# Feed-forward projections as seven products of half matrices instead of eight, in a float32 decoder block

## The chip, the cores and the metric

The kernel runs on one core of a Trainium2 chip. Its metric is the time of one execution on the device, in microseconds (us), as the median of several runs. All data are float32; the tensor engine multiplies them as two float32r parts each, a high one (hi) and the rest (lo).

## The reference

A decoder block for 512 tokens of width 2048: differential attention and a convolution branch, merged by gates; then a feed-forward block of hidden width 5632; then a gated input embedding and a last norm. What the change touches is the feed-forward block and what stands on both sides of it:

```python
        x = x + merged @ w_o[l]
        h = _rmsnorm(x, g_ffn[l])
        u = _causal_dwconv(h @ w_up[l], ffn_conv_w[l], ffn_conv_b[l])
        ug, uv = jnp.split(u, 2, axis=-1)
        x = x + (jax.nn.silu(ug) * uv) @ w_down[l]
        h = _rmsnorm(x, g_ple[l])
        x = x + jax.nn.sigmoid(h @ w_ple_gate[l]) * (p[l].astype(x.dtype) @ w_ple_proj[l])
```

`w_up` is 2048 x 11264, `w_down` 5632 x 2048, and the convolution has three taps along the tokens.

## The kernel before

Activations lie with features on the 128 partitions and the 512 tokens along the free dimension, so a tile is 128 x 512. A weight comes in chunks of 256 x 512 (two blocks of 128 rows side by side, a tile of 128 x 1024 called `wraw`, three buffers). For each chunk `prep` writes the float32r high part with ScalarE (L223, `whi`) and the rest with VectorE (L224, `wlo`, the difference of two tiles in SBUF). Activations are parted the same way by `split` (L118 to L125). A product of a weight block with an activation tile is three matmuls of 512 columns (`products`, L274, L284): hi by hi, hi by lo, lo by hi. A chunk is 2 x 4 such products, so 24 matmuls, into four PSUM banks (`m`).

`run` (L203) walks over all chunks in one order: it issues the load of the chunk three ahead (`LD`), the split of the chunk two ahead (`LP`), then the 24 matmuls, and after a group's last chunk the eviction. Generators that are registered as background work (`add_bg`, `chain`) are pushed on by `pump` once for each chunk. Each engine works through its own queue in order; a scheduler may move instructions a little within it. All DMAs go through SyncE's queue, in the order in which the code issues them (L90).

The feed-forward block (L689 to L752) goes over the hidden width in four parts (`PARTS`). In each part come first the groups of `w_up` (two gate tiles and two value tiles to a group, 8 chunks), then those of `w_down` for that part. `ev_ffn` scales the four banks by the norm's factor (L538), convolves them (L699 once, L701 twice for each tile), applies SiLU (L705), multiplies (L706) and splits the result into the operands of the down products, which stay on chip. `ev_part` adds each part's down product to the residual, on chip too (L718). In all this is 22 groups of 8 chunks for `w_up` and 22 x 4 chunks for `w_down`. The products with `w_proj` stand before the last four down groups. GpSimd does a few constants and a power of a 128 x 4 tile for each norm (L164); nothing else.

Of the kernel before, what the change touches and what calls it, by code (L numbers as in the profile page):

```python
# [31 lines left out]
LD, LP = 3, 2  # chunks that the loads and the splits run ahead  # L32
# [21 lines left out]
class Group:  # L54
    """Products with a block of a weight, K x (128 nm), for the tokens ns; tok: tokens on the output's partitions."""
# [8 lines left out]

class Kernel:
    def __init__(self, tc, ctx, t):
        self.tc, self.nc, self.t = tc, tc.nc, t
        pool = lambda name, bufs, **k: ctx.enter_context(tc.tile_pool(name=name, bufs=bufs, **k))
        self.const = pool("const", 1)
        self.slots = pool("slots", SLOTS)  # L70
        self.wraw = pool("wraw", 3)
# [16 lines left out]

    def load(self, out, in_):
# [25 lines left out]
    # ---- exact split of a float32 tile into two float32r parts  # L115
# [21 lines left out]
    def colsum(self, acc):  # L137
        """[128 feat, 512 tok] -> [128 tok, 4] sums over the partitions."""
# [13 lines left out]
    def colsum_now(self, acc, js):  # L152
        """The same for some of the four blocks, by the shortest way."""
# [6 lines left out]
    def rsqrt(self, ss, scale, eps, n=4):  # L160
# [4 lines left out]
        # one step of Newton's iteration  # L165
# [12 lines left out]
    def bcast(self, r, n=4):  # L178
        """[128 tok, 4] -> [128, 512 tok], the same on every partition."""
# [22 lines left out]
    # ---- the stream of weight chunks  # L202
    def run(self, groups):  # L203
        nc = self.nc
        chunks = [(g, c) for g in groups for c in range(g.n)]
        raws, preps, tiles = {}, {}, {}

        def dma(i, kks=(slice(0, 2),)):
            if i < len(chunks):
                g, c = chunks[i]  # L210
                if i not in raws:
# [3 lines left out]

        def prep(i, kks=(slice(0, 2),)):
            if i >= len(chunks):
                return
            (g, c), raw = chunks[i], raws[i]
            n = g.nm * P  # L220

            def cut(hi, lo, w):
                nc.scalar.activation(hi, w, AF.Copy)  # L223
                nc.vector.tensor_tensor(lo, w, hi.bitcast(F32), op=ALU.subtract)  # L224

# [13 lines left out]
        loadx = self.start(dma, prep)  # L239
        for i, (g, c) in enumerate(chunks):  # L240
            for _ in range(2):
                next(loadx, None)
            dma(i + LD)
            prep(i + LP)
            raws.pop(i, None)
            tiles.pop(i, None)
            if c == 0:
                if g.before:
                    g.before()
# [13 lines left out]
        # the last columns for the other tokens, with the weights that are still here  # L263
        g = self.again
        for m in range(g.nm):
# [6 lines left out]
            g.evict(m, g.ps[m])  # L272

# [12 lines left out]
    # ---- start: the first tiles of x and of the weight, then the constants  # L286
    def start(self, dma, prep):
# [6 lines left out]
        # products of zeros until the first tiles are here: the tensor engine starts at a lower clock  # L294
# [22 lines left out]
        for i in range(1, LD):  # L317
# [38 lines left out]
        # lambda  # L356
# [108 lines left out]
    # ---- conformer convolution  # L465
# [44 lines left out]
    # ---- the whole block  # L510
    def build(self):
# [38 lines left out]
        def heads(h0, z):  # L550
            """The parts of queries and keys, stacked on the partitions: (qh, ql) against (kh, kh) and (kl, kl)."""
# [31 lines left out]
        # gated linear unit of the convolution branch  # L583
# [12 lines left out]
        # gates and branches  # L596
# [49 lines left out]
        # output projection, residual, next norm  # L646
        self.x1, self.hs = {}, {}
        xr = {}

        def load_res(mg):  # L650
            def f():
                if mg == 0:
                    self.finish_chains()
                for m in range(4 * mg, 4 * mg + 4):
                    xr[m] = self.A()
                    self.load(out=xr[m], in_=t["xT"][:, m, :])
            return f

        def ev_res(src, mg, dst, hs, gcol, last):
            """dst = src + product; its squares, and its split times the next norm's gain."""  # L660
            def chain():
                for m in range(4 * mg, 4 * mg + 4):
                    self.nacc = self.square_add(dst[m], self.nacc)
                    hs[m] = self.split(dst[m], self.col(gcol + m))
                    yield
                if mg == 3:
                    yield from last()
            def f(ps):
                for m in range(4):
                    z = src[4 * mg + m]  # L670
                    nc.vector.tensor_tensor(z, ps[m], z, op=ALU.add)  # L671
# [201 lines left out]
```

## Time and profile before

| | us |
|---|---|
| median of 3 runs (2853.17 to 2853.89) | 2853.4 |
| span of the profiled execution | 2851.3 |
| busy: TensorE (PE), its weight loads (PEld) | 2833.7, 2354.3 |
| busy: VectorE (DVE), ScalarE (ACT), GpSimd (POOL) | 1427.3, 907.9, 16.8 |
| feed-forward stretch of the chain that ended last | 1223.8 to 2671.1 |

The span goes from the first to the last instruction on the core; the profiled execution has no time of its own beside it, and the median lies 2.1 us above it. Times of parts of the kernel are read within the span. An engine's busy time is a sum of its instructions' durations, in which overlaps count once; a matmul's own duration (388 ns) is longer than the distance to the next one, since matmuls overlap in the array, so the rate is read from stretches of the chain.

### The profile page before, as it was taken

What the parts mean: (1) busy time and instruction counts of PE and PEld (TensorE: products, weight loads), DVE (VectorE), ACT (ScalarE), POOL (GpSimd) and SP (SyncE); (2) the same over time, 40 slices, a digit from 0 to 9 for tenths busy, and PEclk for the clock granted to TensorE, in tenths of its full rate; (3) what the DMA queues carried; (4) which work ended last, traced back from release to release, by engine and by line L of the source; (5) the groups of instructions that cost most, each with busy time, mean ns of one, the idle gap of its engine ahead of it and who ended that gap; (6) DMA issues with size and microseconds to landing.
All of it is one profiled execution on the core that took longest, in us unless ns stands there. A gap on an engine that the chain in (4) does not pass through costs nothing.

```text
span 2851.3 us, 31442 instructions
## 1 busy us (share of the span) xinstructions
PE 2833.7 (99%) x12824; PEld 2354.3 (83%) x12824; DVE 1427.3 (50%) x2035; ACT 907.9 (32%) x1291; POOL 16.8 (1%) x24
## 2 busy tenths in 40 slices
PE   9999999999999999999999999999999999999997
PEld 7888888888888888888888888888888888888887
DVE  5564687578455443445543345433445433455535
ACT  5354542222133222323321223221233212235333
POOL 0000000000000000000000000000000000000000
PEclk9999999999999999999999999999999999999999
DMA  5333322222222233322222222232222222223232
GB/s 191 111 104 104 97 81 96 96 96 97 97 95 96 98 126 116 112 96 97 96 97 96 96 96 97 98 99 98 96 96 96 96 96 97 97 96 108 94 109 82
DMA packets 86721, 288.27 MB, mean 101 GB/s; under 512 B 9776, under 2 KB 13872, under 8 KB 86576
## 3 DMA queue, kind: packets, MB, share of 16 engines
q1 hardware_dynamic: 86432, 286.25, 30.5%
q8 instruction: 100, 1.64, 0.2%
q14 instruction: 45, 0.37, 0.0%
q10 hardware_dynamic: 144, 0.01, 0.0%
HBM read 275.74 MB, written 4.19 MB: 98 GB/s over the span
## 4 chain that ended last, share of the span: by engine, by line
PE 99%; DMA 0%; DVE 0%; SPq 0%; ACT 0%; issue 0%; POOLq 0%; POOL 0%; DVEq 0%; ACTq 0%
PE m L284 97%; PE x L420 1%; PE x L393 0%; PE x L394 0%; PE x L411 0%; DMA wraw<-w_in 0%; PE x L132 0%; PE x L436 0%; DMA out<-o 0%; SPq L90 0%; DVE o L795 0%; PE x L188 0%; DVE wlo L224 0%; PE x L157 0%; ACT whi L223 0%
## 5 line engine op out<-in xcount | busy, mean ns | idle before, releaser
L284 PE MATMUL m<-a,whi 128*128 128x512 f32 (+1 forms) x7840 | 2403.7, 388 | 0.0
L284 PEld LDWEIGHTS m<-a,whi 128*128 128x128 f32 x7840 | 1467.0, 188 | 300.4 <-DVE a L538 0.3
L284 PE MATMUL m<-a,wlo 128*128 128x512 f32 (+1 forms) x3920 | 1520.0, 388 | 0.0
L224 DVE TENSOR_TENSOR wlo<-wraw,whi 128x1024 fp32r<-128x1024 f32 (+1 forms) x504 | 616.0, 1222 | 1207.7 <-ACT whi L223 1183.1
L223 ACT ACTIVATE whi<-wraw 128x1024 fp32r<-128x1024 f32 (+1 forms) x504 | 533.1, 1058 | 1657.1 <-PE m L284 1511.4
L284 PEld LDWEIGHTS m<-a,wlo 128*128 128x128 f32 x3920 | 736.0, 188 | 151.0 <-DVE wlo L224 0.3
L477 DVE SCALAR_TENSOR_TENSOR a<-a,par 128x485 f32<-128x485 f32 (+19 forms) x240 | 172.5, 733 | 6.1 <-ACT a L474 1.6
L538 DVE TENSOR_TENSOR a<-m,a 128x512 f32<-128x512 f32 x152 | 102.9, 691 | 52.4 <-PE m L284 52.4
L701 DVE SCALAR_TENSOR_TENSOR a<-a,par 128x510 f32<-128x510 f32 (+1 forms) x176 | 120.0, 744 | 0.0
L284 PE MATMUL m<-whi,a 128*128 128x512 f32 x256 | 81.2, 391 | 0.0
L120 ACT ACTIVATE a<-a 128x512 fp32r<-128x512 f32 x88 | 54.4, 620 | 45.1 <-DVE a L175 23.6
L699 ACT ACTIVATE a<-a,par 128x512 f32<-128x512 f32 x88 | 66.3, 801 | 0.0
L121 DVE TENSOR_TENSOR a<-a 128x512 fp32r<-128x512 f32 x88 | 60.2, 686 | 7.6 <-ACT a L120 7.0
L284 PEld LDWEIGHTS m<-whi,a 128*128 128x128 f32 x256 | 48.1, 189 | 10.2 <-ACT whi L223 0.6
L705 ACT ACTIVATE a<-a 128x512 f32<-128x512 f32 x44 | 27.9, 633 | 82.5 <-DVE a L701 82.5
L284 PE MATMUL m<-wlo,a 128*128 128x512 f32 x128 | 50.0, 390 | 0.2 <-DVE wlo L224 0.2
L398 ACT ACTIVATE a<-a,sm 128x128 f32<-128x128 f32 (+3 forms) x64 | 35.4, 554 | 19.8 <-DVE sm L396 19.8
L718 DVE TENSOR_TENSOR a<-m,a 128x512 f32<-128x512 f32 x48 | 32.8, 692 | 15.7 <-PE m L284 15.7
L199 DVE TENSOR_TENSOR a<-a 128x512 f32<-128x512 f32 x52 | 35.7, 686 | 4.7 <-ACT a L198 4.0
L198 ACT ACTIVATE a<-a 128x512 f32<-128x512 f32 x52 | 31.4, 620 | 20.2 <-DVE a L671 19.7
L396 DVE CUSTOM_DVE_ANT_0 a<-x,a 128x128 f32<-128x128 f32 (+3 forms) x64 | 28.9, 487 | 15.6 <-PE x L394 15.0
L706 DVE TENSOR_TENSOR a<-a 128x512 f32<-128x512 f32 x44 | 30.5, 693 | 5.7 <-ACT a L705 1.4
(108 smaller groups left out, 764.0 us busy)
## 6 DMA issues: line engine op xcount, KB each, us to landing
wraw<-w_up SPq DMA_DIRECT2D x176, 512.0 KB, 3.3
wraw<-w_in SPq DMA_DIRECT2D x143, 512.0 KB, 3.3
wraw<-w_down SPq DMA_DIRECT2D x88, 512.0 KB, 3.3
wraw<-w_o SPq DMA_DIRECT2D x32, 512.0 KB, 3.3
wraw<-w_gate SPq DMA_DIRECT2D x32, 512.0 KB, 3.3
a<-xT SPq DMA_DIRECT2D x32, 256.0 KB, 4.7
wraw<-w_attn SPq DMA_DIRECT2D x16, 512.0 KB, 3.3
wraw<-w_conv SPq DMA_DIRECT2D x16, 512.0 KB, 3.3
```

The lines of the kernel that those rows point to most:

```text
L120: nc.scalar.activation(hi, src, AF.Copy)
L121: nc.vector.tensor_tensor(lo, src, hi.bitcast(F32), op=ALU.subtract)
L199: nc.vector.tensor_tensor(acc, acc, q, op=ALU.add)
L223: nc.scalar.activation(hi, w, AF.Copy)
L224: nc.vector.tensor_tensor(lo, w, hi.bitcast(F32), op=ALU.subtract)
L284: nc.tensor.matmul(out, lhsT=l, rhs=r, start=first and n == 0, stop=last and n == 2)
L398: nc.scalar.activation(e[:, :w], e[:, :w], AF.Exp, scale=-1.0, bias=nm[:, c:c + 1], accum_out=sums[:, c:c + 1])
L477: nc.vector.scalar_tensor_tensor(y[:, s:], u[:, :S - s], self.col(w + k), y[:, s:], op0=ALU.mult, op1=ALU.add)
L538: nc.vector.tensor_tensor(a, ps, rb, op=ALU.mult)
L699: nc.scalar.activation(y, u, AF.Identity, scale=self.col(w + 2), bias=self.col(C_FB + ch))
L701: nc.vector.scalar_tensor_tensor(y[:, s:], u[:, :S - s], self.col(w + 2 - s), y[:, s:], op0=ALU.mult, op1=ALU.add)
L718: nc.vector.tensor_tensor(z, ps[m], z, op=ALU.add)
```

## The change

For each product of a 2 x 2 block matrix with a 2 x 2 block activation the change forms seven block products instead of eight (Strassen's method). The four weight blocks are two halves of the inner width by two blocks of 128 outputs: the gate tile and the value tile of a `w_up` column, or two neighbouring output tiles of `w_down`. The four activation blocks are two halves of the inner width by two halves of 256 tokens. Such a unit is a `Pair`, of which there are 44 for `w_up` and 8 in each of the four parts of `w_down`, each of seven steps. `kh` is the number of 128-row blocks in a half: 8 for `w_up`, 6, 6, 5 and 5 for the parts of `w_down`.

Both sides need sums. The weights' sums are made for each pair on GpSimd (`sums`, four additions of 128 x 128 kh, two steps ahead of the pair). The activations' sums are made once by `operands` (four on GpSimd, then seven splits of 256 tokens on ScalarE and VectorE, which put hi in the left and lo in the right half of one tile). A step is for each of the kh blocks one matmul of 512 columns (weight hi by activation hi and lo) and one of 256 columns (weight lo by activation hi). Three PSUM banks hold the seven products; after each step ScalarE copies or VectorE adds a bank into SBUF. The pair's chain folds left and right halves (VectorE), scales `w_up`'s result on GpSimd (L882), and adds `w_down`'s result to the residual on GpSimd (L964).

The operands of `w_up` take more space than before, so all `w_up` pairs come first, and then all parts of `w_down`: the hidden activations go to HBM one by one (`hid`) and come back when a part's operands are built (`builder`, in the last pair ahead of that part). The residual (`x1d`) and the products with `w_proj` (`pjd`, now directly behind `w_o`) go through HBM too. The operands of the first half of `w_o`'s outputs are built beside `w_o`, the rest (`later`) beside `w_proj`. The splits for `w_gate` are now issued at the first `w_gate` group.

```diff
+AHEAD, LP, LA = 16.0, 2, 4
+ORDER = [1, 2, 6, 5, 7, 3, 4]
-PARTS = [12, 12, 12, 8]
+PARTS = [12, 12, 10, 10]
-SLOTS = 80
+SLOTS = 78
+RAWS = 8
...
+    def operands(self, T, q, b1, b2):
+        def put(p, src, sign=1.0):
+            t = T[p][q] = self.A(F32R)
+            if sign == 1.0:
+                nc.scalar.activation(t[:, LEFT], src, AF.Copy)
+                nc.vector.tensor_tensor(t[:, RIGHT], src, t.bitcast(F32)[:, LEFT], op=ALU.subtract)
...
+        nc.gpsimd.tensor_tensor(u[:, LEFT], b1[:, LEFT], b1[:, RIGHT], op=ALU.subtract)
+        nc.gpsimd.tensor_tensor(v[:, LEFT], u[:, LEFT], b2[:, RIGHT], op=ALU.add)
+        nc.gpsimd.tensor_tensor(u[:, RIGHT], b2[:, RIGHT], b1[:, RIGHT], op=ALU.subtract)
+        nc.gpsimd.tensor_tensor(v[:, RIGHT], v[:, LEFT], b2[:, LEFT], op=ALU.subtract)
+        put(1, b1[:, LEFT])
...
+        def sums(i):
+            add = lambda o, x, y: nc.gpsimd.tensor_tensor(o, x, y, op=ALU.add)
+            if c == 2:
+                a11, a21, a22 = g.raw[0], g.raw[2], g.raw[3]
+                s1 = g.raw[4] = self.wraw.tile([P, g.kh, P], F32, tag="w", name="wraw")
+                add(s1, a21, a22)
+                add(a21, a21, a11)
+                add(a11, a11, s1)
+            elif c == 5:
+                add(g.raw[1], g.raw[1], g.raw[0])
...
+            if isinstance(g, Pair):
+                hi = self.whi.tile([P, g.kh, P], F32R, tag="w", name="whi")
+                lo = self.wlo.tile([P, g.kh, P], F32R, tag="w", name="wlo")
+                cut(hi, lo, g.raw[{1: 0, 2: 1, 6: 0, 5: 4, 7: 2, 3: 1, 4: 3}[ORDER[c]]])
...
+        for k in range(g.kh):
+            t = g.rhs(p, k)
+            nc.tensor.matmul(ps, lhsT=hi[:, k], rhs=t, start=new and k == 0, stop=False, skip_group_check=True)
+            nc.tensor.matmul(ps[:, LEFT], lhsT=lo[:, k], rhs=t[:, LEFT], start=False, stop=k == g.kh - 1, skip_group_check=True)
+        if p in (1, 6, 5, 4):
+            x = g.c[p] = self.A()
+            nc.scalar.activation(x, ps, AF.Copy)
+        elif p == 2:
+            nc.vector.tensor_tensor(g.c[1], ps, g.c[1], op=ALU.add)
...
+                    nc.vector.tensor_tensor(u[:, LEFT], l[:, LEFT], l[:, RIGHT], op=ALU.add)
+                    nc.vector.tensor_tensor(u[:, RIGHT], r[:, LEFT], r[:, RIGHT], op=ALU.add)
+                    nc.gpsimd.tensor_tensor(u, u, rb, op=ALU.mult)
...
+                nc.vector.tensor_tensor(yg, yg, yv, op=ALU.mult)
+                hid[j] = self.D(f"hid{j}")
+                self.load(out=hid[j], in_=yg)
...
+                for c in (c11, c12, c21, c22):
+                    fold(c, nc.vector)
...
+                        nc.gpsimd.tensor_tensor(x[:, half], x[:, half], c[:, LEFT], op=op)
```

In the `w_up` stage TensorE's queue held, before, only matmuls of 512 columns:

```order
L284 MATMUL m<-a,wlo 128x512
L284 MATMUL m<-a,whi 128x512 x2
L284 MATMUL m<-a,wlo 128x512
L284 MATMUL m<-a,whi 128x512 x2
L284 MATMUL m<-a,wlo 128x512
```

and it holds now, at the same place:

```order
L389 MATMUL m<-a,whi 128x512
L390 MATMUL m<-a,wlo 128x256
L389 MATMUL m<-a,whi 128x512
L390 MATMUL m<-a,wlo 128x256
L389 MATMUL m<-a,whi 128x512
```

Three matmuls of 512 columns for each weight block and tile have become one of 512 and one of 256 columns for each block and step.

GpSimd's queue ended, before, with the powers of the norms (L164). In the middle of the `w_up` stage it now holds, with the tiles' numbers (`wraw` a weight block or a sum, `a_10723` and `a_10754` the folded results of a pair):

```order
L302 TENSOR_TENSOR wraw_10680<-wraw_10628,wraw_10630 128x1024
L302 TENSOR_TENSOR wraw_10628<-wraw_10628,wraw_10575 128x1024
L302 TENSOR_TENSOR wraw_10575<-wraw_10575,wraw_10680 128x1024
L882 TENSOR_TENSOR a_10723<-a_10723,a_9427 128x512
L302 TENSOR_TENSOR wraw_10604<-wraw_10604,wraw_10575 128x1024
L882 TENSOR_TENSOR a_10754<-a_10754,a_9432 128x512
L302 TENSOR_TENSOR wraw_10867<-wraw_10815,wraw_10817 128x1024
```

The first six rows are one pair's share and the seventh begins the next pair's; all six are new, and each reads two tiles in SBUF.

VectorE's queue in the same stage, with the tiles' numbers (`wlo` the lo part for a step, `a<-m` a bank added up, L880 and L881 the folds, L887 the convolution):

```order
L272 TENSOR_TENSOR wlo_12877<-wraw_12661,whi_12876 128x1024
L272 TENSOR_TENSOR wlo_12900<-wraw_12687,whi_12899 128x1024
L397 TENSOR_TENSOR a_12897<-m_12792,a_12897 128x512
L272 TENSOR_TENSOR wlo_12921<-wraw_12819,whi_12920 128x1024
L399 TENSOR_TENSOR a_12870<-m_12880,a_12870 128x512
L272 TENSOR_TENSOR wlo_12946<-wraw_12848,whi_12945 128x1024
L880 TENSOR_TENSOR a_12967<-a_12809 128x256
L881 TENSOR_TENSOR a_12967<-a_12870 128x256
L272 TENSOR_TENSOR wlo_12976<-wraw_12819,whi_12975 128x1024
L887 SCALAR_TENSOR_TENSOR a_12968<-a_12967,par_149,a_12968 128x511
```

Where before one difference of 128 x 1024 stood for each chunk (24 matmuls), one now stands for each step (8 matmuls of 512 and 8 of 256 columns), with the pair's folds, additions and convolution between.

## Rows read from the trace of the kernel before

**Rows 1.** The page: busy time by engine, and the chain that ended last.

```profile
PE 2833.7 (99%) x12824; PEld 2354.3 (83%) x12824; DVE 1427.3 (50%) x2035; ACT 907.9 (32%) x1291; POOL 16.8 (1%) x24
...
PE 99%; DMA 0%; DVE 0%; SPq 0%; ACT 0%; issue 0%; POOLq 0%; POOL 0%; DVEq 0%; ACTq 0%
```

**Rows 2.** Chain in order of time: start, us, what; the feed-forward block.

```profile
1223.81 1447.25 PE m L284 x6384
```

**Rows 3.** Chain in order of time: the last columns' matmuls of 256, and last multiplications.

```profile
2819.01 15.36 PE m L284 x128
...
2841.32 2.09 DVE o L795 x6
```

**Rows 4.** Groups by shape, 1223.81 to 2671.06: xcount | busy, mean ns | idle before.

```profile
L284 PEld LDWEIGHTS m<-a,whi 128*128 128x128 f32 x4255 | 798.6, 188 | 165.8
...
L224 DVE TENSOR_TENSOR wlo<-wraw,whi 128x1024 fp32r<-128x1024 f32 x266 | 326.0, 1226 | 762.4 <-ACT whi L223 762.4
L223 ACT ACTIVATE whi<-wraw 128x1024 fp32r<-128x1024 f32 x267 | 282.8, 1060 | 920.0 <-PE m L284 902.9 <-issue 15.1 <-ACT a L123 2.0
L699 ACT ACTIVATE a<-a,par 128x512 f32<-128x512 f32 x88 | 66.3, 801 | 0.0
...
L121 DVE TENSOR_TENSOR a<-a 128x512 fp32r<-128x512 f32 x47 | 32.0, 685 | 1.4 <-ACT a L120 1.4
...
L705 ACT ACTIVATE a<-a 128x512 f32<-128x512 f32 x44 | 27.9, 633 | 82.5 <-DVE a L701 82.5
...
L735 ACT ACTIVATE a<-m 128x512 f32<-128x512 f32 x16 | 9.5, 593 | 6.0 <-PE m L284 5.4
```

**Rows 5.** DVE in order of time, 1325 to 1336: start, us, instruction.

```profile
1325.16 2.73 DVE L538 TENSOR_TENSOR a<-m,a 128x512 f32<-128x512 f32 x4 [1.31 <-PE m L284]
1328.07 1.23 DVE L224 TENSOR_TENSOR wlo<-wraw,whi 128x1024 fp32r<-128x1024 f32 x1 [0.18 <-ACT whi L223]
1329.21 2.73 DVE L701 SCALAR_TENSOR_TENSOR a<-a,par 128x511 f32<-128x511 f32 x4
...
1334.65 0.68 DVE L121 TENSOR_TENSOR a<-a 128x512 fp32r<-128x512 f32 x1
1335.25 2.73 DVE L701 SCALAR_TENSOR_TENSOR a<-a,par 128x511 f32<-128x511 f32 x4
```

**Rows 6.** POOL in order of time: constants, and four of its twelve 128x4 powers.

```profile
1.60 0.10 POOL L328 MEMSET mhalf<- 128x4 f32 x1
...
2.29 0.61 POOL L355 TENSOR_SCALAR_AFFINE_SELECT dist<-dist 128x512 f32<-128x512 f32 x1
...
259.20 1.01 POOL L164 TENSOR_TENSOR sm<-sm,mhalf 128x4 f32<-128x4 f32 x1 [24.49 <-DVE sm L163]
...
367.16 1.37 POOL L164 TENSOR_TENSOR sm<-sm,mhalf 128x4 f32<-128x4 f32 x1 [31.83 <-DVE sm L163]
392.28 1.35 POOL L164 TENSOR_TENSOR sm<-sm,mhalf 128x4 f32<-128x4 f32 x1 [23.75 <-DVE sm L163]
417.12 1.37 POOL L164 TENSOR_TENSOR sm<-sm,mhalf 128x4 f32<-128x4 f32 x1 [23.50 <-DVE sm L163]
```

**Rows 7.** DVE at the same four moments.

```profile
258.89 0.16 DVE L163 TENSOR_SCALAR sm<-sm 128x4 f32<-128x4 f32 x1
260.24 0.16 DVE L166 SCALAR_TENSOR_TENSOR sm<-sm 128x4 f32<-128x4 f32 x1 [1.18 <-POOL sm L164]
...
366.91 0.75 DVE L477 SCALAR_TENSOR_TENSOR a<-a,par 128x505 f32<-128x505 f32 x1
...
392.04 0.72 DVE L477 SCALAR_TENSOR_TENSOR a<-a,par 128x487 f32<-128x487 f32 x1
...
416.88 0.74 DVE L477 SCALAR_TENSOR_TENSOR a<-a,par 128x507 f32<-128x507 f32 x1
```

**Rows 8.** Busy time by engine (x instructions), granted clock, DMA share, GB/s, feed-forward and end.

```profile
1223.81:2671.06 1447.25, 1447.25 (x6385) 1198.12 (x6385) 623.57 (x716) 422.34 (x496) 0.00 (x0) 1.00 0.29 97
...
2835.00:2851.00 16.00, 1.80 (x6) 1.02 (x6) 7.88 (x25) 1.08 (x3) 0.69 (x1) 0.62 0.40 131
```

**Rows 9.** DMA issues: what, count, KB each, median us to landing.

```profile
wraw<-w_up SPq DMA_DIRECT2D x176, 512.0 KB, 3.3
```

More of the change, by code (lines that the diff above doesn't have):

```diff
@@ L206, in run, with cut @@
         raws, preps, tiles = {}, {}, {}
+        begun = set()
+        work = [g.kh * 0.347 if isinstance(g, Pair) else 1.36 * g.nm for g, _ in chunks]
+        def cut(hi, lo, w):
+            nc.scalar.activation(hi, w, AF.Copy)
+            nc.vector.tensor_tensor(lo, w, hi.bitcast(F32), op=ALU.subtract)
         def dma(i, kks=(slice(0, 2),)):
@@ L214, in dma, with loads @@
                     self.load(out=raws[i][:, kk, :g.nm * P], in_=g.w[c][:, kk])
+        def loads(i):
+            t, j = 0.0, i + 1
+            while j < len(chunks) and t < AHEAD and j < i + 7:
+                if j not in begun:
+                    begun.add(j)
+                    dma(j)
+                t += work[j]
+                j += 1
+        def sums(i):
+            if i >= len(chunks) or not isinstance(chunks[i][0], Pair):
+                return
+            g, c = chunks[i]
+            add = lambda o, x, y: nc.gpsimd.tensor_tensor(o, x, y, op=ALU.add)
[7 more added lines that the diff above has]
+                add(g.raw[1], g.raw[1], g.raw[0])
         def prep(i, kks=(slice(0, 2),)):
@@ L316, in start @@
             load(k)
-        for i in range(1, LD):
+        for i in range(1, 3):
             dma(i)
@@ new lines, in build, with builder, fetch @@
+        Tp = [{p: {} for p in ORDER} for _ in PARTS]
+        F0 = [sum(PARTS[:i]) for i in range(len(PARTS))]
+        builders = [None] * len(PARTS)
+        def builder(pi):
+            n = PARTS[pi] // 2
+            b = {}
+            def fetch(q):
+                if q < n:
+                    for f in (F0[pi] + q, F0[pi] + n + q):
+                        b[f] = self.A()
+                        self.load(out=b[f], in_=hid[f])
+            fetch(0)
+            yield
+            for q in range(n):
+                fetch(q + 1)
+                for _ in self.operands(Tp[pi], q, b[F0[pi] + q], b[F0[pi] + n + q]):
+                    pass
+                yield
@@ new lines, in build, with ev_down, chain, f @@
+        for j in range(KF):
+            last = j == KF - 1
+            groups.append(Pair(t["w_up"][j], lambda p, k: T2[p][k], ev_up(j),
+                               before=first_up if j == 0 else begin(0) if last else None,
+                               after=build(0) if last else None))
+        def ev_down(pi, mg):
+            def chain(c11, c12, c21, c22):
+                for c in (c11, c12, c21, c22):
+                    fold(c, nc.vector)
+                yield
+                for m, l, r, op in ((2 * mg, c11, c12, ALU.add), (2 * mg + 1, c21, c22, ALU.subtract)):
+                    x = self.x1[m]
+                    for half, c in ((LEFT, l), (RIGHT, r)):
+                        nc.gpsimd.tensor_tensor(x[:, half], x[:, half], c[:, LEFT], op=op)
+                    yield
+            def f(*c):
+                self.finish_chains()
+                self.chain(chain(*c))
+            return f
@@ new lines, in build, with split_x1 @@
+        for pi, n in enumerate(PARTS):
+            for mg in range(8):
+                last = pi + 1 < len(PARTS) and mg == 7
+                groups.append(Pair(t[f"w_down{pi}"][mg], lambda p, k, pi=pi: Tp[pi][p][k], ev_down(pi, mg),
+                                   before=ready(pi, mg), after=build(pi + 1) if last else None))
+        h2, pj = {}, {}
+        def split_x1():
+            for k in range(KD):
+                if k == KD - 2:
+                    self.finish_chains()
+                h2[k] = self.split(self.x1[k], self.col(C_GPLE + k))
+                self.nacc = self.square_add(self.x1[k], self.nacc)
+                if k % 2:
+                    yield
+            yield from stats("rb3")()
@@ L755, in ev_gate2, with begin_gate, load_pj, f @@
+        def begin_gate():
+            self.g_split = self.add_bg(split_x1())
+            next(self.g_split)
+            next(self.g_split)
+        def load_pj(mg):
+            def f():
+                if mg == 0:
+                    begin_gate()
+                for m in range(4 * mg, 4 * mg + 4):
+                    pj[m] = self.A()
+                    self.load(out=pj[m], in_=pjd[m])
+            return f
         def ev_gate2(m0, ns=ALL):
```

246 lines of the change are left out of this document (170 added, 76 removed).

## The prediction

> **What bounds the kernel now.** I read the page first: TensorE is busy 99% of the span and makes 99% of the chain that ended last [rows 1], so only what shortens TensorE's work, or makes it wait, moves the time. Next the chain in order of time: the feed-forward block is one unbroken run of 6384 matmuls in 1447.25 us [rows 2], 226.7 ns for each matmul of 512 columns. The same chain has a run of matmuls of 256 columns, 128 in 15.36 us [rows 3], 120.0 ns each. So the weight load, whose own duration is 188 ns [rows 4], lies beside other work even at 120 ns, and a matmul costs about 13 ns beside its columns. Then the stretch by engine: in these 1447 us VectorE is busy 624, ScalarE 422 and GpSimd 0 us [rows 8], so the helpers have room now, and the question is whether they keep it. Last, for what the change puts on VectorE and GpSimd, their instructions in order of time [rows 5 to 7].
>
> **What TensorE saves.** Before, `w_up` is 22 x 8 x 24 = 4224 and `w_down` 22 x 4 x 24 = 2112 matmuls of 512 columns: 6336 x 0.2267 = 1436.4 us. After, `w_up` has 44 x 7 x 8 = 2464 and `w_down` 8 x 7 x (6+6+5+5) = 1232 steps of one 512 and one 256 matmul: 3696 x (0.2267 + 0.1200) = 1281.4 us. Saved: 155.0 us. `w_proj` and everything else keep their matmuls. A `w_up` pair is then 56 x 0.3467 = 19.41 us of TensorE, a `w_down` pair 14.56 us (kh 6) or 12.13 us (kh 5).
>
> **What VectorE must do in that time.** I count by distance from start to start, as instructions overlap a little. A difference of 1024 columns takes 1.14 us (1328.07 to 1329.21), one of 512 takes 0.60 (1334.65 to 1335.25), a convolution tap 2.73 / 4 = 0.68, an addition from PSUM 0.68 [rows 5]; one of 256 columns 2.09 / 6, about 0.34 [rows 3]; between, 0.87 for 768 and 0.74 for 640 columns. A `w_up` pair: 7 x 1.14 + 4 folds x 0.34 + 4 taps x 0.68 + 0.60 = 12.66 us with both inputs in SBUF, and 3 x 0.68 = 2.05 from PSUM; 14.7 of 19.41 fits. A `w_down` pair: 7 x 0.87 + 4 x 0.34 = 7.45 (kh 6) or 6.54 (kh 5), and 2.05. ScalarE in a `w_up` pair: 7 x 1.06 + 4 x 0.59 + 2 x 0.80 + 0.63 = 12.0 us [rows 4]; fits, and costs nothing while it does.
>
> **What GpSimd must do.** The trace has no addition there. The lower bound for 1024 columns is VectorE's instruction of the same form, 1.23 us [rows 4, 5]. The upper bound is GpSimd's own one-input row: 0.61 us for 512 columns [rows 6]; two inputs of 1024 read four times as much, at most 4 x 0.61 = 2.45 us. I take the same engine's row, less a fixed part as in its shortest row, 0.10 us [rows 6]: 0.51 for 512 columns read, so 0.10 + 4 x 0.515 = 2.16 us for 1024, 1.13 for 512, 1.65 for 768, 1.39 for 640, 0.61 for 256. A `w_up` pair: 4 x 2.16 + 2 x 1.13 = 10.9 us; a `w_down` pair 4 x 1.65 + 4 x 0.61 = 9.04 or 8.0 us. Alone, all of it fits too.
>
> [...]
>
> **Whether both fit at once** decides the case. Nine of GpSimd's twelve powers of a 128 x 4 tile took 1.01 us, as the one at 259.20; three took 1.35 to 1.37 [rows 6]. In those three, and only there, VectorE was inside an instruction with two inputs in SBUF, which had begun 0.24 us before: 366.91 + 0.75, 392.04 + 0.72 and 416.88 + 0.74 are its ends, and the power ended 0.87 us behind the end each time [rows 6, 7]; at 259.20 VectorE was idle until 260.24 [rows 7]. So an instruction that reads four elements stood still until VectorE's was over. I take it that the two exclude each other, in both directions; the rows show only GpSimd's side.
>
> [...]
>
> Then these times add up. `w_up` pair: 12.66 + 10.9 = 23.56 against 19.41, 4.15 us lost, x 44 = 183 us. `w_down`: 7.45 + 9.04 = 16.49 against 14.56, 1.93 x 16 = 31 us; 6.54 + 8.0 = 14.54 against 12.13, 2.41 x 16 = 39 us. VectorE's additions from PSUM have one SBUF input and I let them lie beside GpSimd; if they don't, a `w_up` pair costs up to 2.05 us more (90 us in all).
>
> **Building a part's operands.** `operands` is, for each q, 7 x 0.34 = 2.4 us on VectorE and 4 x 0.61 = 2.44 us on GpSimd. For the four parts it stands in the last pair before the part, with its first step needing all q: (6+6+5+5) = 22 times 4.82 us, beside a pair that is already over its time: 106 us. Before, the same tiles were split one by one beside the products. Without exclusion VectorE alone is the bound there: 14.7 + 6 x 2.4 - 19.41, 9.5 + 6 x 2.4 - 14.56, 9.5 + 5 x 2.4 - 14.56 and 8.6 + 5 x 2.4 - 12.13, in all 34 us.
>
> **Smaller moves.** Four q of `w_up`'s operands beside `w_proj` (96 matmuls, 21.8 us): 19.3 us of exclusive work, about 4.6 of `w_proj`'s own splits and some statistics; 10 us late, between 0 and 20. The first `w_gate` split now comes directly behind the last pair: about 4 us. Together 14.
>
> **New waits.** ScalarE's L885 waits for GpSimd's L882, and behind it stand the bank copies for which TensorE's next step on that bank waits; this is how GpSimd's lateness reaches TensorE, and it is in the sums above. SyncE's store of `hid` waits for VectorE's L892, and behind it stand four weight loads; they run some 16 us ahead and land in 3.3 us [rows 9], so it costs nothing while the buffers are free; without that cover up to 3.3 us a pair, 145 us. HBM traffic grows by 76 tiles of 0.26 MB out and in, 40 MB; DMA is at 0.29 of its time there [rows 8]: nothing.
>
> **The sum.** 2851.3 - 155.0 + 183 + 31 + 39 + 106 + 14 = 3069.3 us of span, and with the 2.1 us that the median lies above it 3071. With GpSimd at 2.45 us for 1024 columns the losses are 242 + 43 + 48 + 106 + 14 = 453 and the time 3151; at 1.70 us about 2900.
>
> **The rivals.**
> First, no exclusion that counts: GpSimd only waits at its start, or VectorE never waits for it. Then everything fits beside TensorE but the operands: 2853.4 - 155 + 34 + 8 = 2740 us, faster. For it speaks that each engine alone has room and that VectorE's side is not in the rows; against it the three delays that end with VectorE's instruction. It decides as soon as a `w_up` pair's sum stays under 19.41 us.
> Second, exclusion, but short additions: at the lower bound (1.23 us, 0.69 for 512 columns, 0.42 for 256) a `w_up` pair takes 12.66 + 6.3 = 19.0, under 19.41; only the operands stay, (2.4 + 1.7) x 22 less the room in these pairs, 85, and 14: 2797 us, faster. The two sides meet at about 1.55 us for 1024 columns. Against it speaks GpSimd's 0.61 for one input of half the length.
> Third, the seventh does not come: the short matmul doesn't cover the weight load, and a step costs two loads, 2 x 188 = 376 instead of 346.7 ns. 3696 x 0.029 = 108 us on top of the first rival: 2848 us, no change. The 120.0 ns of rows 3 speak against it.
>
> **How the numbers follow.** The forecast, exclusion with additions from about 1.6 us up: 0.58, 2900 to 3170 (the upper end is 2.45 us and part of the 90 us). First rival 0.25; second 0.13, of which 0.02 lies within 0.2% of 2853.4; third 0.04, of which I put 0.03 on no change and 0.01 on faster. A measurement of this kernel tells about 0.2% from no change. So faster 0.37, same 0.05, slower 0.58. With both signs this strong the range reaches over both: leaving out half of the first rival below and a little above, 2740 to 3170 us.
>
> **What will show it.** If right: `wlo` (L272) has a mean far above 1.23 us, or VectorE's idle time before it ends with GpSimd; additions L302 of 2.2 us alone and longer beside VectorE; TensorE busy about 83% in the `w_up` stage with waits for `wlo`, and a pair at 23 to 24 us; longer gaps at the four part changes, about 25 us each. If the first rival is right, a pair takes 19.4 us and L272 keeps its 1.23. Each step of 16 matmuls should take 2.77 us wherever nothing is late. The forecast is wrong if additions are short, if VectorE passes GpSimd, or if gaps let TensorE's clock fall: the granted clock is 1.00 in the feed-forward stretch and 0.62 in the nearly idle last 16 us [rows 8]; I expect gaps of a few us at most between busy steps, and no fall.

## The result, and the profile after

| | before | after |
|---|---|---|
| median of the runs, us | 2853.4 | 3300.2 (3296.1 to 3303.7) |
| ratio to before, 95% interval | | 1.1565 (1.1549 to 1.1581) |
| span of the profiled execution, us | 2851.3 | 3296.1 |
| mean granted TensorE clock, whole span | 0.998 | 0.931 |

The change makes the kernel slower by 447 us. The prediction had the direction right (3071, slower), but it worked out a loss of 218 us, and the time lies above its range of 2740 to 3170 us.

The page of the changed kernel: busy time by engine, TensorE's granted clock in 40 slices of the span, the chain that ended last by engine, and three of the costliest groups.

```profile
PE 2861.6 (87%) x13880; PEld 2377.2 (72%) x13880; DVE 2371.7 (72%) x2841; ACT 1314.7 (40%) x2022; POOL 1168.1 (35%) x664
...
PEclk9999999999999999889888988888887989889998
...
PE 6%; DVE 1%; issue 0%; ACT 0%; POOL 0%; POOLq 0%; DVEq 0%; ACTq 0%
...
L272 DVE TENSOR_TENSOR wlo<-wraw,whi 128x1024 fp32r<-128x1024 f32 (+3 forms) x772 | 1062.8, 1381 | 556.8 <-ACT whi L271 530.5
...
L302 POOL TENSOR_TENSOR wraw<-wraw 128x1024 f32<-128x1024 f32 (+2 forms) x304 | 727.0, 2391 | 621.9 <-DMA wraw<-w_up 480.5
...
L882 POOL TENSOR_TENSOR a<-a 128x512 f32<-128x512 f32 x88 | 145.0, 1647 | 72.1 <-DVE a L881 71.8
```

Against [rows 1], TensorE is no longer busy all the time; its busy time even grew, from 2833.7 to 2861.6 us, though 155 us of matmuls were taken away: in the stretch of the feed-forward block its granted clock is 0.89 (1223 to 2928 us), where [rows 8] had 1.00. The chain that ended last can be followed back over 7% of the span only, so what follows is read from windows, from the waits and from instructions in order of time. The differences L272 take 1.38 us on average against 1.23 in [rows 4], although a part of them is shorter now, and GpSimd, which has the additions (L302), stands idle for 481 us waiting for weights.

One stretch of the `w_up` stage in the windows view: busy time (x instructions) of TensorE, its weight loads, VectorE, ScalarE and GpSimd, then granted clock, DMA share, GB/s.

```profile
1300.00:2100.00 800.00, 620.69 (x3118) 515.58 (x3117) 602.85 (x531) 315.16 (x390) 394.43 (x168) 0.87 0.23 83
```

No engine is the bound there: VectorE is busy 75%, GpSimd 49%, TensorE 78% at 0.87 of its clock. The time goes to waits of one for the other. TensorE's waits over the whole span (engine, line, releaser: us in total, times, longest):

```profile
PE m L389 <- ACT a L393: 123.1, 49, 12.1
PE m L389 <- ACT whi L271: 117.0, 38, 8.0
PE m L390 <- DVE wlo L272: 114.4, 73, 4.1
```

How long a unit takes I read from VectorE's addition behind the sixth of a pair's seven steps (L399): the first and the 43rd start of the `w_up` stage.

```profile
1252.28 0.68 DVE L399 TENSOR_TENSOR a<-m,a 128x512 f32<-128x512 f32 x1
...
2448.34 0.69 DVE L399 TENSOR_TENSOR a<-m,a 128x512 f32<-128x512 f32 x1 [0.57 <-PE m L390]
```

That is (2448.34 - 1252.28) / 42 = 28.48 us for a pair, against 23.56 in the prediction and 96 x 0.2267 = 21.76 us for the same work before. In the same way, from starts three pairs apart in the part with kh 6 and four apart in one with kh 5,

```profile
2580.32 0.68 DVE L399 TENSOR_TENSOR a<-m,a 128x512 f32<-128x512 f32 x1
2629.56 0.68 DVE L399 TENSOR_TENSOR a<-m,a 128x512 f32<-128x512 f32 x1
...
2870.11 0.68 DVE L399 TENSOR_TENSOR a<-m,a 128x512 f32<-128x512 f32 x1
2927.20 0.68 DVE L399 TENSOR_TENSOR a<-m,a 128x512 f32<-128x512 f32 x1
```

a `w_down` pair takes 16.4 us (kh 6; predicted 16.49) and 14.3 us (kh 5; predicted 14.54), and the pairs around the four part changes exceed these by 37.8, 27.5, 23.3 and 23.3, in all 112 us (predicted 106). So one term is wrong: the `w_up` pair, by 4.9 us, 44 times, 216 of the 229 us that are missing. The experiments look for these 4.9 us.

### The profile page after: what moved, and what is told of

Same layout as the page of the kernel before. It is cut to its first block, busy times and chain, and to the rows that moved or that the text cites. A ratio compares the mean times of both kernels' runs of the same rounds, so it can differ in the third digit from the quotient of the medians.

```text
span 3296.1 us, 36977 instructions
## 1 busy us (share of the span) xinstructions
PE 2861.6 (87%) x13880; PEld 2377.2 (72%) x13880; DVE 2371.7 (72%) x2841; ACT 1314.7 (40%) x2022; POOL 1168.1 (35%) x664
## 5 line engine op out<-in xcount | busy, mean ns | idle before, releaser
L389 PE MATMUL m<-a,whi 128*128 128x512 f32 x3696 | 1415.4, 422 | 271.6 <-ACT a L393 123.1
L272 DVE TENSOR_TENSOR wlo<-wraw,whi 128x1024 fp32r<-128x1024 f32 (+3 forms) x772 | 1062.8, 1381 | 556.8 <-ACT whi L271 530.5
L271 ACT ACTIVATE whi<-wraw 128x1024 fp32r<-128x1024 f32 (+3 forms) x772 | 750.6, 978 | 1338.6 <-PE m L415 615.4
L390 PE MATMUL m<-a,wlo 128*128 128x256 f32 x3696 | 1084.2, 295 | 115.3 <-DVE wlo L272 114.4
L415 PE MATMUL m<-a,whi 128*128 128x512 f32 (+1 forms) x3616 | 1107.7, 388 | 16.6 <-ACT a L851 13.1
L302 POOL TENSOR_TENSOR wraw<-wraw 128x1024 f32<-128x1024 f32 (+2 forms) x304 | 727.0, 2391 | 621.9 <-DMA wraw<-w_up 480.5
L390 PEld LDWEIGHTS m<-a,wlo 128*128 128x128 f32 x3696 | 744.6, 201 | 151.6 <-DVE wlo L272 149.5
L415 PEld LDWEIGHTS m<-a,whi 128*128 128x128 f32 x3616 | 676.1, 188 | 154.3 <-ACT a L851 13.5
L415 PE MATMUL m<-a,wlo 128*128 128x512 f32 (+1 forms) x1808 | 699.9, 387 | 0.0
L224 POOL TENSOR_TENSOR sm<-sm,mhalf 128x4 f32<-128x4 f32 (+1 forms) x14 | 14.6, 1042 | 1060.9 <-DVE sm L223 1060.9
L415 PEld LDWEIGHTS m<-a,wlo 128*128 128x128 f32 x1808 | 340.7, 188 | 69.0
L887 DVE SCALAR_TENSOR_TENSOR a<-a,par 128x511 f32<-128x511 f32 (+1 forms) x176 | 201.8, 1147 | 146.0 <-ACT a L885 145.6
L964 POOL TENSOR_TENSOR a<-a 128x256 f32<-128x256 f32 x128 | 173.4, 1358 | 45.4 <-DVE a L868 42.9
L882 POOL TENSOR_TENSOR a<-a 128x512 f32<-128x512 f32 x88 | 145.0, 1647 | 72.1 <-DVE a L881 71.8
L168 POOL TENSOR_TENSOR a<-a 128x256 f32<-128x256 f32 x30 | 33.6, 1120 | 306.5 <-DVE a L812 230.5
L881 DVE TENSOR_TENSOR a<-a 128x256 f32<-128x256 f32 x88 | 130.6, 1484 | 0.0
L880 DVE TENSOR_TENSOR a<-a 128x256 f32<-128x256 f32 x88 | 106.9, 1215 | 0.2
```

The source lines that it names most:

```text
L302: add = lambda o, x, y: nc.gpsimd.tensor_tensor(o, x, y, op=ALU.add)
L389: nc.tensor.matmul(ps, lhsT=hi[:, k], rhs=t, start=new and k == 0, stop=False, skip_group_check=True)
L390: nc.tensor.matmul(ps[:, LEFT], lhsT=lo[:, k], rhs=t[:, LEFT], start=False, stop=k == g.kh - 1, skip_group_check=True)
L415: nc.tensor.matmul(out, lhsT=l, rhs=r, start=first and n == 0, stop=last and n == 2)
L881: nc.vector.tensor_tensor(u[:, RIGHT], r[:, LEFT], r[:, RIGHT], op=ALU.add)
L882: nc.gpsimd.tensor_tensor(u, u, rb, op=ALU.mult)
```

## The experiments

"Pair" is the mean distance of `w_up` pairs as above, "clock" the granted clock from 1300 to 2100 us, which is inside the `w_up` stage in all of them but the kernel before, where `w_up` and `w_down` take turns.

| kernel | what | median, us | ratio to before (95%) | pair, us | clock |
|---|---|---|---|---|---|
| before | | 2853.4 | 1 | 21.76 | 1.00 |
| after | the change | 3300.2 | 1.1565 (1.1549 to 1.1581) | 28.48 | 0.87 |
| e1 | `hid` stored a pair later | 3239.9 | 1.1351 (1.1334 to 1.1368) | 27.12 | 0.92 |
| e2 | weight sums on VectorE | 3075.7 | 1.0784 (1.0766 to 1.0802) | 24.68 | 0.92 |
| e3 | both | 2937.4 | 1.0294 (1.0279 to 1.0309) | 21.44 | 1.00 |
| e4 | before, with additions on GpSimd | 2854.0 (one run) | | | |
| e5 | e1, writes in place of the sums | 2888.1 | 1.0123 (1.0108 to 1.0138) | 20.85 | 1.00 |
| e6 | e1, TensorE kept busy in its gap | 3178.6 | 1.1139 (1.1123 to 1.1156) | 25.63 | 1.00 |
| v1 | e3 for `w_up`, plain `w_down` | 2864.2 | 1.0036 (1.0023 to 1.0049) | 21.43 | 1.00 |
| v2 | v1, halves added in PSUM | 2808.0 | 0.9839 (0.9823 to 0.9856) | 20.16 | 1.00 |
| v3 | v2, 80 tiles instead of 78 | 2798.3 | 0.9807 (0.9791 to 0.9823) | 20.16 | 1.00 |

**Theory** from these readings: VectorE and GpSimd do exclude each other as predicted, but GpSimd starts late on top of it, since its weights come late; and TensorE's gaps lower its clock. **Rivals**: GpSimd's instructions are simply longer than assumed, and nothing else is wrong; or what counts is not the exclusion at all but the order of GpSimd's queue, behind which everything waits.

### e4: does each side really stop the other?

```diff
+            if g in marked:
+                o = self.scr.tile([P, 2, S], F32, tag="o", name="scr")
+                nc.gpsimd.tensor_tensor(o, hi.bitcast(F32), raw, op=ALU.add)
```

in the kernel before, for 96 chunks of `w_up`, with a result that nobody reads.

> The kernel before with one addition of 128 x 1024 on GpSimd more for each of 96 w_up chunks, of the chunk and its high part, into a tile that nobody reads (80 tiles and the smaller descriptor store kept as they allow). TensorE is the bound there, so the time may stay. Exclusion in both directions: wherever one begins while the other runs, its duration grows by what is left of the other: additions of 2.4 us alone become about 3.5 behind a difference of 1.23, and VectorE's instructions that begin inside an addition take up to 2.4 us more. Exclusion in one direction: VectorE's stay at 1.23, 0.75 and 0.69. No exclusion: the additions stay at 2.4 as well.

GpSimd, then VectorE, in order of time at one place of e4 (start, us, instruction, idle time before):

```profile
1379.69 3.38 POOL L242 TENSOR_TENSOR scr<-whi,wraw 128x1024 f32<-128x1024 f32 x1 [3.68 <-ACT whi L225]
...
1394.40 2.55 POOL L242 TENSOR_TENSOR scr<-whi,wraw 128x1024 f32<-128x1024 f32 x1 [0.80 <-ACT whi L225]
```

```profile
1379.60 1.23 DVE L226 TENSOR_TENSOR wlo<-wraw,whi 128x1024 fp32r<-128x1024 f32 x1 [0.25 <-ACT whi L225]
1380.74 2.89 DVE L122 TENSOR_TENSOR a<-a 128x512 fp32r<-128x512 f32 x1
```

The addition that begins 0.09 us behind VectorE's difference takes 3.38 us. None of the 96 runs alone (the shortest takes 2.48 us), but some additions of the changed kernel do. Here are two, one behind the other, while VectorE has nothing to do:

```profile
1564.11 4.84 POOL L302 TENSOR_TENSOR wraw<-wraw 128x1024 f32<-128x1024 f32 x2 [12.99 <-DMA wraw<-w_up]
```

That is 2.4 us for each; the 17 beside which VectorE runs nothing take 2.35 to 2.40. In e4, VectorE's next difference, 0.69 us by itself, stands behind the addition and takes 2.89. From the end of VectorE's first (1380.83) to the end of the addition (1383.07) are 2.24 us: this long VectorE is shut out. So the exclusion holds in both directions, and the first rival of the prediction (it doesn't count) is out. Four additions at 2.24 us instead of the predicted 2.16 are 0.3 of the 4.9 us, so that they are simply longer is out, too. The kernel's time doesn't move (2854.0 against 2853.4 us), since VectorE has the room there that [rows 8] show.

### e1: the store that stood ahead of the loads

In the changed kernel, SyncE's instructions and GpSimd's around one pair:

```profile
1696.04 0.33 SPq L117 DMA_DIRECT2D hid<-a  x1
1696.46 1.82 SPq L117 DMA_DIRECT2D wraw<-w_up  x4
```

```profile
1688.44 1.70 POOL L882 TENSOR_TENSOR a<-a 128x512 f32<-128x512 f32 x1 [0.36 <-DVE a L881]
1702.96 8.94 POOL L302 TENSOR_TENSOR wraw<-wraw 128x1024 f32<-128x1024 f32 x3 [12.82 <-DMA wraw<-w_up]
```

The four loads go out the moment the store of `hid` has gone, so their buffers were free; the store had waited for VectorE's last multiplication of the pair (L892; over all pairs SyncE waits 1157.7 us for it, 44 times). GpSimd stands idle for 12.8 us and then begins when the weights land. e1 issues each store one pair later, when its tile is long ready:

```diff
-                self.load(out=hid[j], in_=yg)
+                late.append((hid[j], yg))
...
             def f(*c):
                 self.finish_chains()
+                store_late()
                 self.chain(chain(*c))
```

> One part changed: the store of a pair's hidden tile is issued one pair later, so that the four weight loads behind it no longer wait for that pair's last multiplication. Theory A (two causes: exclusion of VectorE and GpSimd, and loads held up behind the store): additions L302 no longer wait for DMA, a w_up pair falls from 28.5 to about 25 us (12.7 us of two-input VectorE work and 4 x 2.4 + 2 x 1.25 of GpSimd), w_down pairs stay at 16.4 and 14.3; about 3140 us. Rival B (the loads are not on the path; the pair is long because the in-order queues of ScalarE and VectorE wait for GpSimd and TensorE's clock falls): within 30 us of 3300.

Measured 3239.9, 60 us less: between the two numbers and nearer to the rival's. GpSimd's wait for weights went from 480.5 to 17.1 us, but another one took its place. GpSimd's waits in e1:

```profile
POOL wraw L302 <- DVE wlo L272: 427.6, 125, 9.1
```

The sums are made in place, over blocks that an earlier step's split must have read first; where GpSimd is no longer held up by the loads, it is held up there. So the store is one cause, worth 60 us alone, and not the main one.

### e2 and e3: the sums on VectorE

```diff
-            add = lambda o, x, y: nc.gpsimd.tensor_tensor(o, x, y, op=ALU.add)
+            add = lambda o, x, y: nc.vector.tensor_tensor(o, x, y, op=ALU.add)
```

e2 is this alone, e3 this and the edit of e1.

> One part changed: the four weight additions of a pair go to VectorE. Theory A: VectorE then has 19.3 us of its own in a w_up pair and GpSimd 2.5, with the loads still late: pair 23 to 25 us, w_down pairs at TensorE's 14.6 and 12.1 or 0.5 above; about 3030 us. Rival C (VectorE is simply overloaded, without exclusion): 4.6 us more on it makes a pair longer than 28.5 us, and the kernel slower than 3300.

> Both changes of the two runs before. Theory A: w_up pair 21 to 22 us, w_down pairs at TensorE's time, the four part changes still some 25 us each: about 2940 us. Rival B: as with the additions on VectorE alone. Rival C: slower than 3300.

e2 comes to 3075.7, 45 us above what I expected: its loads were still late, which I had counted in, and its clock stayed at 0.92, of which I had said nothing; the pair, 24.68 us, lies at the high side of my 23 to 25, and which of the two holds the 45 us was not tried. e3 comes to 2937.4 as expected. VectorE does an addition in 1.22 us for which GpSimd shuts it out for 2.24, so an engine that is already the fuller one wins by taking over the work of the emptier one. On top of that, the late store costs 3075.7 - 2937.4 = 138 us, where it cost 60 us before, with the fall of the clock in it (0.92 in e2, 1.00 in e3): here the same wait is worth more when less else is late.

### e5: is it the reading?

```diff
-            add = lambda o, x, y: nc.gpsimd.tensor_tensor(o, x, y, op=ALU.add)
+            def add(o, x, y):
+                for _ in range(2):
+                    nc.gpsimd.memset(o, 0.01)
```

> The kernel of e1 (store one pair later), with each of the four weight additions of a pair replaced by two GpSimd writes of a constant over the same tile: same place in the queue, same waits, same readers, but nothing is read from SBUF. The weight sums are left out, so five of the seven products take other weights. Theory A (VectorE and GpSimd cannot read SBUF at the same time): VectorE's instructions take their bare times beside these writes (L272 about 1.23 us on average, against 1.38 in the changed kernel), a w_up pair needs 12.7 + 2.3 us exclusive plus 2.05, so TensorE is the bound again, a pair takes 19.5 to 20.5 us and the whole about 3240 - 44 x 7 = 2930 us. Rival B (what costs is that GpSimd's queue is late, and everything behind it waits): the writes are in the same queue behind the same waits, a pair stays at 25 us or more and the whole at 3140 us or more.

GpSimd and VectorE in e5 at one place:

```profile
1500.10 3.65 POOL L304 MEMSET wraw<- 128x1024 f32 x4 [0.22 <-DMA wraw<-w_up]
...
1507.07 1.74 POOL L889 TENSOR_TENSOR a<-a 128x512 f32<-128x512 f32 x1 [2.05 <-DVE a L888]
```

```profile
1500.59 0.42 DVE L887 TENSOR_TENSOR a<-a 128x256 f32<-128x256 f32 x1
1500.93 0.42 DVE L888 TENSOR_TENSOR a<-a 128x256 f32<-128x256 f32 x1
1502.32 1.23 DVE L272 TENSOR_TENSOR wlo<-wraw,whi 128x1024 fp32r<-128x1024 f32 x1 [0.97 <-ACT whi L271]
...
1507.57 2.32 DVE L272 TENSOR_TENSOR wlo<-wraw,whi 128x1024 fp32r<-128x1024 f32 x1
```

Beside 3.65 us of writes VectorE's three instructions with two SBUF inputs take their bare times. The fourth stands beside the multiplication with the norm's factor (L889), which still reads two tiles on GpSimd, and takes 2.32. From 1300 to 2100 us, 39 of the 270 differences stand beside that multiplication and take 2.30 to 2.32 us; all others take 1.21 to 1.23, 115 of them beside writes. So their mean is 1.38 and not the 1.23 that I expected, and the same run shows both sides: what reads shuts VectorE out, what writes does not. A write takes 0.96 us, so the eight of a pair 7.7 us, where four additions take 9 to 10: somewhat shorter, but their place in the queue is the same, GpSimd waits as long there for VectorE's differences as in e1 (280.5 us against 270.7, from 1300 to 2100 us), and the pair falls from 27.12 to 20.85 us. The rival of the queue's order is out. The kernel's time, 2888.1, is 42 us below what I expected, although the pair is 0.35 us above the upper end: the weight sums of `w_down` are writes, too, and its pairs take 14.6 to 15.0 and 12.1 to 12.4 us, where the changed kernel's take 16.4 and 14.3. In the changed kernel the same folds look like this beside an addition (VectorE in order of time; compare the 0.41 us of the last row):

```profile
1707.02 2.61 DVE L880 TENSOR_TENSOR a<-a 128x256 f32<-128x256 f32 x1
1709.55 2.62 DVE L881 TENSOR_TENSOR a<-a 128x256 f32<-128x256 f32 x1
...
1717.33 0.41 DVE L880 TENSOR_TENSOR a<-a 128x256 f32<-128x256 f32 x1
```

### e6: what the clock costs

TensorE in e1 around its longest gap of a pair, and after it:

```profile
1704.94 0.48 PE L389 MATMUL m<-a,whi 128*128 128x512 f32 x1
1709.00 0.58 PE L390 MATMUL m<-a,wlo 128*128 128x256 f32 x1 [3.59 <-DVE wlo L272]
...
1713.65 0.41 PE L390 MATMUL m<-a,wlo 128*128 128x256 f32 x1
1713.86 0.52 PE L389 MATMUL m<-a,whi 128*128 128x512 f32 x1
1714.22 0.28 PE L390 MATMUL m<-a,wlo 128*128 128x256 f32 x1
```

and the granted clock there (windows of 2 us, columns as above):

```profile
1704.00:1706.00 2.00, 1.41 (x8) 0.87 (x6) 2.00 (x2) 1.84 (x4) 1.92 (x2) 1.00 0.00 0
1706.00:1708.00 2.00, 0.00 (x0) 0.00 (x0) 2.00 (x1) 0.57 (x2) 1.87 (x1) 0.82 0.00 0
1708.00:1710.00 2.00, 1.00 (x3) 0.90 (x4) 2.00 (x3) 0.00 (x0) 0.00 (x0) 0.50 0.03 8
...
1714.00:1716.00 2.00, 2.00 (x13) 1.76 (x12) 1.71 (x2) 0.95 (x1) 0.00 (x0) 0.97 0.96 389
```

TensorE had nothing to do for 3.6 us; its granted clock fell to 0.50, and the next step took 5.2 us for its eight pairs of matmuls, 0.65 us for each instead of 0.347. e6 puts 14 matmuls into that gap:

```diff
+        if g.kh == 8 and c == 4:
+            fill = self.X()
+            for _ in range(14):
+                nc.tensor.matmul(fill, lhsT=self.onesr, rhs=g.rhs(p, 0), start=True, stop=True)
```

> The kernel of e1 (store one pair later), with 14 matmuls of 512 columns (3.2 us at the full clock) put on TensorE ahead of the fifth step of each w_up pair, the place where it stands still for 3.6 us and then runs at half its clock. They write a spare bank that nobody reads. Theory A (the fall of the clock is a part of the loss of its own): the gap is filled, the granted clock of 1300 to 2300 us rises from 0.92 to 0.98 or more, the steps behind the gap take 2.8 instead of 3.9 to 5.1 us, and the whole falls by 44 times 1.2 to 2.3 us, to 3140 to 3190 us. Rival B (the steps at the low clock lie beside work of VectorE and GpSimd that is late anyway): the clock rises but the time stays within 20 us of 3240. If the gap is not always there, the matmuls cost up to 3.2 us a pair, and it gets slower.

TensorE at that place in a pair of e6, and e6 from 1300 to 2100 us:

```profile
1503.06 3.36 PE L390 MATMUL x<-a,onesr 128*128 128x512 f32 x14
1507.20 0.39 PE L394 MATMUL m<-a,wlo 128*128 128x256 f32 x1 [0.55 <-DVE wlo L272]
```

```profile
1300.00:2100.00 800.00, 736.55 (x3934) 613.79 (x3933) 743.62 (x594) 347.01 (x435) 447.44 (x187) 1.00 0.27 93
```

616 matmuls whose results nobody reads make the kernel 61 us faster: 1.49 us a pair, at the low side of what I expected and more than the rival allows. The clock is 1.00 again, and the pairs are all alike (25.5 to 25.9 us from the second on). Now VectorE is busy, or shut out within an instruction, 743.6 of 800 us: 23.8 of the 25.63 us of a pair, and idle 1.8.

### v1, v2 and v3: a version that gains

```diff
-            nc.tensor.matmul(ps, lhsT=hi[:, k], rhs=t, start=new and k == 0, stop=False, skip_group_check=True)
...
+            for half in (LEFT, RIGHT):
+                nc.tensor.matmul(ps, lhsT=hi[:, k], rhs=t[:, half], start=new and k == 0 and half is LEFT, stop=False, skip_group_check=True)
...
-                    nc.vector.tensor_tensor(u[:, LEFT], l[:, LEFT], l[:, RIGHT], op=ALU.add)
-                    nc.vector.tensor_tensor(u[:, RIGHT], r[:, LEFT], r[:, RIGHT], op=ALU.add)
-                    nc.gpsimd.tensor_tensor(u, u, rb, op=ALU.mult)
...
+                    nc.vector.tensor_tensor(u, u, rb, op=ALU.mult)
```

is the core of v2 (here `ps` is half a bank). v1 is what it starts from: e3's `w_up`, and for `w_down` the plain products and the splits of before, with `hid` read back from HBM.

> The w_up stage of e3 (store late, weight sums on VectorE), but w_down with its eight products as in the kernel before: parts of 12, 12, 12 and 8 hidden tiles, which come back from HBM and are split one by one during the last two groups of the part before. Theory: the w_up pair keeps e3's 21.0 us against 21.76 before (957.6 us for 44), so the w_up stage gains 31 to 33 us; w_down costs what it did before (479 us), without the 112 us at the part changes; w_proj between w_o and w_up costs about 13 us and the change of stage some us. In all 2853 - 32 + 13 + 5 = about 2840 us, between 2830 and 2850, so hardly faster than the kernel before. Rival (the down products themselves, not the part changes, are what e3 loses): 2900 us or more cannot come out of plain products; it would show as waits of the w_down matmuls for hid tiles from HBM.

> v1, and in w_up each step adds the hi and lo halves of the activations in PSUM: three matmuls of 256 columns into one half bank instead of one of 512 and one of 256. The bank copies and additions halve, the folds disappear; the multiplication with the norm's factor and the activations' sums go to VectorE, so GpSimd is out of the feed-forward block. VectorE per pair: 7 x 1.14 + 4 x 1.14 + 3 x 0.34 + 2 x 0.60 + 4 x 0.68 + 0.60 = 18.1 us; TensorE 7 x 8 x 0.360 = 20.2 us. Theory: TensorE is the bound, a pair takes 20.2 to 20.6 us, the whole 2853 - 44 x (1.2 to 1.6) + 10 = 2795 to 2812 us, faster than the kernel before. Rival: VectorE at 90% in order cannot keep ahead of TensorE, a pair takes 21 us or more and the time is 2830 us or more; or a matmul of 256 columns takes over 120 ns when each has its own weights, with TensorE busy throughout.

v1 comes to 2864.2, 24 us above what I expected: I had taken e3's pair as 21.0 us, which its second half shows, but its first 18 pairs take 22.0; 0.43 x 44 = 19 us of the 24. With VectorE busy 787 of 800 us (e3), a pair is there as long as VectorE's own work. Against e3 it shows what the seven products cost in `w_down` with their part changes: 73 us more than the eight. v2 does as expected: TensorE's pair grows by 0.75 us, VectorE's shrinks, and in the windows view TensorE is the bound again.

```profile
1300.00:2100.00 800.00, 800.00 (x6669) 800.00 (x6668) 731.66 (x833) 417.38 (x554) 0.00 (x0) 1.00 0.38 120
```

168 matmuls of 256 columns in 20.16 us are 120.0 ns each, as in [rows 3]. The stage gains 44 x 1.60 = 70 us, the kernel 46. Part of the rest is at the end. TensorE in v2, with the last matmuls of the last columns, and ScalarE a little before:

```profile
2778.88 0.28 PE L419 MATMUL m<-a,wlo 128*128 128x256 f32 x1
2790.95 1.01 PE L217 MATMUL x<-ones,a 128*128 128x1 f32 x4 [11.80 <-DVE a L1013]
```

```profile
2771.36 1.34 ACT L1012 ACTIVATE a<-a 128x256 f32<-128x256 f32 x4 [11.41 <-PE m L419]
```

The gap of 11.8 us was 2.9 in the kernel before, and it stands in the changed kernel, too (11.8 us, ahead of L217 at 3281.27). ScalarE's squares wait for TensorE, whose results they don't read.

```diff
-SLOTS = 78
-RAWS = 8
+SLOTS = 80
+RAWS = 7
```

> v2 with 80 tiles for activations as in the kernel before (the change has 78) and 7 instead of 8 for weights, nothing else. In v2 TensorE stands still for 11.8 us at the end of the last columns, in the kernel before for 2.9; in v2, ScalarE's squares of the first token half wait 11.4 us until TensorE has read a tile. Theory: they wait for a free tile; with two more the wait is gone, the end is 9 us shorter and the whole about 2799 us. Rival: it is the order in which the instructions stand; then the time stays within 2 us of 2808. A buffer less for weights costs nothing if w_up pairs stay at 20.2 us.

2798.3: the gap is 2.8 us now, and the kernel is faster than before by 1.9% (0.9807, 0.9791 to 0.9823).

## Why the prediction was wrong

By its own steps:

- **What TensorE saves**: right. At the full clock a step of 16 matmuls takes 2.77 us in the changed kernel, too (26 times one long and one short matmul from 1702.72 to 1711.73 us, 0.347 us each), and in v2 the matmuls of 256 columns hold 120.0 ns. The third rival falls with that.
- **GpSimd's addition**, 2.16 us: 2.35 to 2.40 alone, and by e4 2.24 during which VectorE is shut out. Nearly right for the sum, which is about VectorE, and inside the bounds of 1.23 and 2.45.
- **Both engines don't fit at once**: right, in both directions (e4), and by the reading (e5). The additions from PSUM, which I let lie beside GpSimd, do: L395, L397 and L399 have means of 678, 688 and 691 ns in the `w_up` stage, against 0.68 us in [rows 5]. The first two rivals fall.
- **The down pairs and the parts' operands**: the down pairs are right, 16.4 and 14.3 against 16.49 and 14.54 us. There the sum of what must not overlap is the time: from 2564 to 2630 us VectorE is busy or shut out for 63.4 of 66 us, at a clock of 1.00. The operands, 112 against 106 us, are right as a number only, and partly by luck: around the part change at 2680 us the clock falls, too (0.56 from 2670 to 2680), which the 106 us leave out, and how the 112 divide was not tried.
- **The `w_up` pair in the sum**: the step that failed. 23.56 us was the sum of what must not overlap, and I took that sum for the time. 28.48 was measured, 4.92 more. By the experiments 1.36 of it goes with the late store (e1, in which the clock rises from 0.87 to 0.92, too), another 1.49 with the clock (e6), and 2.07 us is left in e6. Of these 25.63 us VectorE is busy or shut out for 23.8 and idle for 1.8, in which it waits itself. (By the prediction's times the 23.8 us are 14.7 of its own work, with the 2.05 us of additions from PSUM that my 23.56 left out, and so an estimated 9.1 of being shut out, where the sum had 10.9. That 23.56 + 2.05 comes out at 25.61 is chance: in the changed kernel 21 of 42 first additions and 17 of 42 third ones lie within a GpSimd instruction and take no longer for it, 0.68 and 0.69 us, and in e6 these two have the same 0.68 and 0.69.) I read the 2.07 us as this: two in-order queues that exclude each other and wait for each other's results don't pack without gaps. No run takes them away, so that this is their cause is argued and not shown.
- **New waits**, the store of `hid`: wrong. I let it cost nothing "while the buffers are free" and bounded it by the 3.3 us of a landing, 145 us in all. The buffers were free, and it cost 60 us by itself and 138 us between e2 and e3: under that bound, but not by the landing. The lead of 16 us is counted in the order in which the code issues; in SyncE's queue the four loads stood behind the store and went out 0.42 us after it (1696.04 and 1696.46), so a store that waits for the end of a pair's chain takes that lead away from them.
- **No fall of the clock**: wrong. I expected gaps of a few us and no fall; in e1's rows above it fell to 0.50 in a gap of 3.6 us, and e6 shows what that is worth (61 us, at 1.00 instead of 0.92).
- **Smaller moves**: `w_proj` stands still 13 us (L415, once) where I had 10. Not foreseen at all: the end, 11.8 instead of 2.9 us, from two activation tiles less, or from what else v3 changes with them (a weight buffer); the two were not tried apart.

216 for the `w_up` pairs, 6 for the part changes, 3 for `w_proj`, 9 for the end, and about 5 back from the shorter down pairs come to the 229 us between 3071 and 3300.

Left open: of the 1.8 us that VectorE is idle in e6, how much would go if the sums were not made in place; that wait is the largest before GpSimd's additions in e1 and e6 (427.6 and 366.3 us), but a version with tiles of their own for the sums was not tried.

## What to carry to other kernels

Two engines that exclude each other share one budget: add their times before moving work to the emptier one, take the result as the time only where neither waits for anything else (it was that in the `w_down` pairs, and 4.92 us too little in the `w_up` pairs), and let the faster engine do the work (here 1.22 us an addition on VectorE, and 2.24 of shutting it out on GpSimd). Look at each in-order DMA queue for a store that waits for late results and stands ahead of loads; a lead counted in program order ends at that store (60 us here, and 138 between e2 and e3). And when a wait can stop the matmul stream for some us, price the slower matmuls behind it, too (here a step of 5.2 us instead of 2.77 behind a gap of 3.6).

## What was not expected of the hardware

- It is GpSimd's reading that shuts VectorE out: beside its writes VectorE's instructions with two SBUF inputs stay at 1.23 and 0.42 us, beside a multiplication of the same run 1.23 becomes 2.32 (e5), and an addition makes 0.41 into 2.6 and 0.69 into 2.89 us.
- An instruction that is shut out shows as longer, not as waiting: the folds of 2.6 us above have no idle time before them, and of the 176 folds of the `w_up` pairs one has more than 0.1 us, so VectorE looks busy where it does nothing, and none of its waits names GpSimd's additions.
- 14 matmuls without use, 3.4 us of TensorE's time in each of 44 pairs, paid for themselves 61 us over, by keeping the granted clock at 1.00 instead of 0.92.
